# Splitting one weight unit in four with ScalarE and an adding DMA in a two-layer hybrid trunk

## The chip, the cores and the metric

The kernel runs on one core of one Trainium2 chip. A time is device microseconds of one execution. The profile is of one further execution, taken by the hardware profiler; its times are microseconds from its start. PE is TensorE, DVE is VectorE, ACT is ScalarE, POOL is GpSimd and SP is SyncE. SP, ACT and POOL can issue DMA transfers, which all run on the core's 16 DMA engines.

## What is computed

The reference is a trunk of two layers over 256 tokens of width 2048, all in float32. Each layer has one projection of the normalised input (2048 to 8208 columns), two groups of mixing heads on its results, an output projection, and a gate on a second, small projection:

```python
for l in range(DEPTH):                       # DEPTH = 2, D_MODEL = 2048, SEQ = 256
    hn = rms_norm(h, norm_w[l])
    proj = hn @ w_in[l]                      # 2048 x 8208
    ...
    y = jnp.concatenate([y_a, y_b], axis=-1) # gated DeltaNet heads, HGRN2 heads
    h = h + y @ w_out[l]                     # 2048 x 2048
    gate = jax.nn.sigmoid(h @ w_ple_gate[l]) # 2048 x 2048
    h = h + (p[l] @ w_ple_up[l]) * gate      # 256 x 2048
return rms_norm(h, final_norm_w)
```

## The kernel before

**Products in three parts.** The matmuls use the type float32r, which keeps fewer bits than float32. So each operand x is split into a high part, x rounded to float32r, and a low part, x minus the high part. A product a times w is then the sum of three matmuls: a high by w high, a high by w low, a low by w high (`products`, L414 to L434). All accumulate in PSUM.

**Steps and units.** The weights are packed ahead in the order in which they are used. One step of the plan (`make_plan`, L87) uses one weight unit: mostly two row blocks of 128 rows with 512 columns, which in SBUF are 128 partitions with 1024 float32 each (512 KB). A step is 12 matmuls of 128x512: two row blocks, two halves of 128 tokens, three parts. There are 392 steps, 196 a layer. In layer 0, steps 0 to 127 are the input projection ("in"), 128 to 159 the output projection ("out"), 160 to 195 the gate projection ("gate") with one step of the small projection ("up") in each of its four chunks of 512 columns. Layer 1 is the same from step 196 on. The first two chunks of a stage take turns, four row blocks each; the third and fourth follow one after the other.

**How a unit is made.** `load` (L374) lets SP issue the transfer from HBM into a tile `raw` of the pool `wraw` (three buffers). `prep` (L387) lets ACT write the high part `whi` (L400) and DVE the low part `wlo` (L402), into pools of three buffers each. `ahead` (L405) runs in program order before each step n: it asks for loads up to four units ahead, limited to three more than have been prepared, and for parts up to two units ahead. So ACT can write unit n's high part when the step three units earlier has been done, and a `raw` buffer comes free when DVE has read it.

**What sets the order.** The matmuls and transposes on PE are kept in the program's order. On the other engines a scheduler orders the instructions when the program is built; each engine then works through its own queue in that order, waiting on semaphores. After each step the mixing heads' next pieces are run from a table of delays (`tick`, L358), and those of `after_out` (L1163) and `after_gate` (L1169) when a chunk of the out or gate stage is done. `after_gate` makes the sigmoid of a chunk's gate on ACT and DVE (L1172, L1174, L1176, L1177), adds to h on DVE (L1179, L1180) and takes sums of squares on ACT (L555). In the last layer POOL multiplies h by the final norm's weight (L1183).

**Buffers that the change borrows.** The pool `mix` has a tag "et" (two tiles of 1024 float32 on each partition), which holds the evicted results of the input projection until they are transposed (`evict`, L593), and at the start the transposed input. Its tag "Bt" (one tile of 2048) holds the matrices of the DeltaNet heads that are inverted (`Inverse`, L612). Neither is written between the end of one input projection's work and the next one.

Of the kernel before, what the change touches and what calls it, by code (L numbers as in the profile page):

```python
# [8 lines left out]
F32 = mybir.dt.float32  # L9
F32R = mybir.dt.float32r  # L10
I32 = mybir.dt.int32
AF = mybir.ActivationFunctionType
ALU = mybir.AluOpType
# [18 lines left out]
def chunk_cols(chunk):  # L32

    return [(START[k], 16) if k == "ba" else (START[k] + 256 * g, 256) for k, g in chunk]
# [52 lines left out]
def make_plan():  # L87

    steps, off = [], 0

    def add(what, l, c, cols, k, first, last):
        nonlocal off
        n = sum(w for _, w in cols)
        steps.append(dict(what=what, l=l, c=c, cols=cols, n=n, kts=k, off=off, first=first, last=last))
        off += 128 * n * len(k)

    for l in range(DEPTH):
        for what in ("in", "out", "gate"):
            chunks, order = stage_plan(what, l)
            for c, k4 in order:  # L100
                cols = chunk_cols(chunks[c]) if what == "in" else [(512 * c, 512)]
                w = 2 if sum(x for _, x in cols) > 272 else 4
                kts = OUT_KTS if what == "out" else tuple(range(KT))
                for q in range(0, 4, w):
                    last = k4[q + w - 1] == kts[-1]
                    end = l + 1 == DEPTH and c == 3
                    if what == "gate" and k4[q + w - 1] == KT - (9 if end else 1):
                        add("up", l, c, cols, (0, 1), True, True)
                    add(what, l, c, cols, k4[q:q + w], k4[q] == kts[0], last)
    return steps, off  # L110
# [56 lines left out]
def trunk(ctx: ExitStack, tc: tile.TileContext, head, xT, x, pT, W, par, fw, cst, msk, eye, out):  # L167
    nc = tc.nc
# [7 lines left out]
    mp = pool("mix", 1)  # L176
# [4 lines left out]
    V, S, G = nc.vector, nc.scalar, nc.gpsimd  # L181
# [187 lines left out]
    steps, _ = make_plan()  # L369
    raws, ready = {}, {}  # L370
    LOOK, LOAD = 2, 4
    state = dict(next=0, loaded=0, prepped=0)

    def load(n, after=None):  # L374
        s = steps[n]
        f = s["n"] * len(s["kts"])
        raw = raws[n] = wr.tile([128, 1088], F32, tag="raw", name=f"raw{n}")
        i = nc.sync.dma_start(out=raw[:, :f], in_=W[s["off"]:s["off"] + 128 * f].rearrange("(p f) -> p f", p=128))
        if n <= 17:
            tc.keep_in_program_order(i)  # L380
        if after is not None:
            tc.add_manual_dep(i.ins, after.ins.name, mybir.DependencyInfo(
                mybir.DependencyClass.Sync, mybir.DependencyReason.DATA), reason="later")
        if n in follow:
            follow[n]()

    def prep(n):  # L387
        s = steps[n]
        f = s["n"] * len(s["kts"])
        raw = raws.pop(n)  # L390
        if n >= len(steps) - 2:

            ready[n] = [split(raw[:, 512 * j:512 * j + 512], j, None, f"w{n}") for j in range(2)]
            return
        hi = ws.tile([128, 1088], F32R, tag="whi", name=f"whi{n}")
        lo = ws.tile([128, 1088], F32R, tag="wlo", name=f"wlo{n}")
        w = f // 4 if n < 2 else f
        parts = [slice(j, j + w) for j in range(0, f, w)]
        for sl in parts:
            S.activation(hi[:, sl], raw[:, sl], AF.Copy)  # L400
        for sl in parts:
            V.tensor_tensor(lo[:, sl], raw[:, sl], hi[:, sl].bitcast(F32), ALU.subtract)  # L402
        ready[n] = [(hi[:, j * s["n"]:(j + 1) * s["n"]], lo[:, j * s["n"]:(j + 1) * s["n"]]) for j in range(len(s["kts"]))]

    def ahead(n):  # L405
        while state["loaded"] < min(len(steps), n + 1 + LOAD) or state["prepped"] < min(len(steps), n + 1 + LOOK):
            if state["loaded"] < min(len(steps), n + 1 + LOAD, state["prepped"] + WRAW):
                load(state["loaded"])
                state["loaded"] += 1
            else:  # L410
                prep(state["prepped"])
                state["prepped"] += 1

    def products(n, m, psums, act, js=range(4), run=None, parts=range(3)):  # L414

        s = steps[n]
        if isinstance(psums[m], list):
            if run is None:
                products(n, m, psums, act, run=0)
                run = 1  # L420
            ps, cols = psums[m][run], RUNS[run]
        else:
            ps, cols = psums[m], slice(0, s["n"])
        for j, (hi, lo) in enumerate(ready[n]):
            if j not in js:
                continue
            kp, kj = divmod(s["kts"][j], 2)
            ah, al = (a[:, T * kj + 128 * m:T * kj + 128 * m + 128] for a in act[kp])
            o = ps[:, cols]
            for i, (a, b) in enumerate(((ah, hi), (ah, lo), (al, hi))):  # L430
                if i not in parts:
                    continue
                PE.matmul(o, a, b[:, cols], start=(s["first"] and j == 0 and i == 0),
                          stop=(s["last"] and j == len(ready[n]) - 1 and i == 2))  # L434

    def run_step(psums, act):

        n = state["next"]
        s = steps[n]
        ahead(n)  # L440
        if not n:
            for j in range(4):
                for i in (0, 2, 1):
                    for m in range(2):
                        products(n, m, psums, act, js=(j,), parts=(i,))
                if j == 1:
                    warm(1)
        for m in range(2):
            if n:
                products(n, m, psums, act)  # L450
        del ready[n]
        state["next"] = n + 1
        if s["what"] != "up":
            tick()
        return s
# [25 lines left out]
    def split(src, kp, scales, name):  # L481

        hi = ap_.tile([128, 2 * T], F32R, tag="ahi", name=f"{name}hi{kp}")
        lo = ap_.tile([128, 2 * T], F32R, tag="alo", name=f"{name}lo{kp}")
        if scales is None:
            S.activation(hi, src, AF.Copy)
            V.tensor_tensor(lo, src, hi.bitcast(F32), ALU.subtract)
            return hi, lo
        w = 2 * T // len(scales)
        for j, sc in enumerate(scales):  # L490
            S.activation(hi[:, w * j:w * j + w], src[:, w * j:w * j + w], AF.Copy, scale=sc)
        for j, sc in enumerate(scales):
            sl = slice(w * j, w * j + w)
            V.scalar_tensor_tensor(lo[:, sl], src[:, sl], sc, hi[:, sl].bitcast(F32), ALU.mult, ALU.subtract)
        return hi, lo
# [762 lines left out]
    for l in range(DEPTH):  # L1258
# [25 lines left out]
        for c, k4 in order:  # L1284
# [5 lines left out]
            w = 2 if sum(n for _, n in chunk_cols(ch)) > 272 else 4  # L1290
            for q in range(0, 4, w):
# [19 lines left out]
                s = run_step(ps[c], act)  # L1311
# [28 lines left out]
        for c, k4 in order:  # L1340
            if c not in ps:
                ps[c] = banks(f"gate{l}{c}", c)
                if l + 1 == DEPTH and c == 3:

                    ps[c][1] = [ps[c][1], pm.tile([128, 512], F32, tag="m", name="gaterun")]
            for q in (0, 2):
                end = l + 1 == DEPTH and c == 3
                if k4[q + 1] == KT - (9 if end else 1):
                    up = [pm.tile([128, 512], F32, tag="m", name=f"up{l}{c}{m}") for m in range(2)]
                    run_step(up, pact)  # L1350
                if end and k4[q + 1] == KT - 9:
                    break
                while not pairs_ready(hact, k4[q:q + 2]):
                    tick()
                run_step(ps[c], hact)
            if end and k4[3] == KT - 9:

                n = state["next"]
                for i in range(5):
                    ahead(n + i)  # L1360
                    products(n + i, 0, ps[c], hact)
                half0 = Finish(0, ps[c], up, st)
                for r in range(2):
                    for i in range(5):
                        products(n + i, 1, ps[c], hact, run=r)
                last_norm(half0, Finish(1, ps[c], up, st))
                break
            if k4[3] == KT - 1:
                spawn(after_gate(c, ps[c], up, act, st, l))
# [35 lines left out]
```

## Time and profile before

| what | value |
|---|---|
| three runs | 1246.13 us median, 1245.79 to 1248.45 |
| the profiled execution, first to last instruction | 1246.4 us; no other time of its own is given |
| mean granted TensorE clock | 0.996 |
| busy: PE, DVE, ACT, POOL | 1229.5, 880.0, 778.1, 69.5 us |
| out and gate stages of layer 0, in the trace | about 428 to 623 us |
| out and gate stages of layer 1, in the trace | about 1044 to 1237 us |
| bytes moved by DMA | 218.71 MB, 175 GB/s in the mean |

A group of instructions in the profile is a line with its engine, its operation and the tiles out<-in, the count after an x, then the busy time in us and the mean of one in ns, then the idle time of that engine just before them with what ended it. A row of the timeline has the start, the duration, the engine, the line and the operation. A row of the chain of waits has the start, the duration, and the engine and tile that the end of the program depended on in that time. Rows of a table by stretches have the busy time of PE, weight loads, DVE, ACT and POOL, the granted clock, the busy share of the DMA engines and GB/s.

### The profile page before, as it was taken

The page shows a single profiled execution, that of the slowest core. Times are in us where ns is not written, and L with a number is a line of the kernel's source. Part 1 is how long each engine was busy: PE and PEld are TensorE (multiplying, and loading weights), DVE is VectorE, ACT ScalarE, POOL GpSimd, SP SyncE. Part 2 cuts the span into 40 slices and gives each one's busy share as a digit, 9 for nine tenths or more (in the row PEclk, how much of TensorE's full clock was granted, in tenths as well). Part 3 has the DMA queues.
Part 4 walks back from the last instruction along what each step waited for, and adds up shares of the span by engine and source line. Part 5 has one row for each costly group of instructions (what it writes and reads, how often), then busy time and mean ns, then how long its engine had stood idle before and what let it go on. Part 6 is the DMA issues. An engine that isn't in the chain of part 4 may idle for free.

```text
span 1246.4 us, 21626 instructions
## 1 busy us (share of the span) xinstructions
PE 1229.5 (99%) x8385; PEld 1033.1 (83%) x8385; DVE 880.0 (71%) x1520; ACT 778.1 (62%) x1397; POOL 69.5 (6%) x64
## 2 busy tenths in 40 slices
PE   9999999999999999999999999999999999999996
PEld 7888887798888888888888888887888888888886
DVE  7777796878568656547567778977876695565566
ACT  7676776586757744437556768674766576444464
POOL 0310000000000000000003100000000000000010
PEclk9999999999999999999999999999999999999998
DMA  8555555435464445555555555555445555656563
GB/s 288 174 178 175 174 174 160 170 122 187 152 219 153 170 177 184 187 186 186 187 184 170 174 178 165 177 175 154 134 140 165 172 156 185 207 179 181 183 203 135
DMA packets 73719, 218.71 MB, mean 175 GB/s; under 512 B 15504, under 2 KB 20752, under 8 KB 73616
## 3 DMA queue, kind: packets, MB, share of 16 engines
q1 hardware_dynamic: 63392, 211.78, 52.0%
q10 hardware_dynamic: 10224, 5.54, 1.5%
q8 instruction: 66, 1.08, 0.3%
q14 instruction: 37, 0.30, 0.1%
HBM read 212.84 MB, written 4.46 MB: 174 GB/s over the span
## 4 chain that ended last, share of the span: by engine, by line
PE 89%; DVE 6%; ACT 2%; DMA 1%; issue 1%; SPq 0%; DVEq 0%; ACTq 0%
PE out L336 14%; PE gate L336 14%; PE in1hf L336 7%; PE in0dk L336 7%; PE in0dv L336 6%; PE in1dv L336 6%; PE in1dk L336 6%; PE in1hi L336 6%; PE in0hf L336 5%; PE in0hi L336 4%; DVE wlo L402 2%; PE up L336 2%; PE in1dz L336 1%; PE in0dz L336 1%; ACT whi L400 1%
## 5 line engine op out<-in xcount | busy, mean ns | idle before, releaser
L402 DVE TENSOR_TENSOR wlo<-raw,whi 128x1024 fp32r<-128x1024 f32 (+1 forms) x392 | 483.0, 1234 | 273.9 <-ACT whi L400 272.7
L400 ACT ACTIVATE whi<-raw 128x1024 fp32r<-128x1024 f32 (+1 forms) x392 | 411.6, 1051 | 328.2 <-PE out L336 90.8
L336 PE MATMUL in1hf<-whi,n1hi 128*128 128x512 f32 x128 | 51.0, 398 | 0.9 <-issue 0.9
L336 PE MATMUL in1hi<-whi,n1hi 128*128 128x512 f32 x128 | 51.6, 403 | 0.0
L336 PE MATMUL in1dk<-whi,n1hi 128*128 128x512 f32 x128 | 51.3, 401 | 0.0
L336 PE MATMUL in1hi<-wlo,n1hi 128*128 128x512 f32 x128 | 50.0, 391 | 0.7 <-DVE wlo L402 0.7
L336 PE MATMUL gate<-whi,g0hi 128*128 128x512 f32 x128 | 50.1, 392 | 0.0
L336 PE MATMUL in1dk<-wlo,n1hi 128*128 128x512 f32 x128 | 50.0, 391 | 0.1
L336 PE MATMUL in1hi<-whi,n1lo 128*128 128x512 f32 x128 | 50.0, 391 | 0.0
L336 PE MATMUL in1dk<-whi,n1lo 128*128 128x512 f32 x128 | 50.0, 390 | 0.0
L336 PE MATMUL in1hf<-whi,n1lo 128*128 128x512 f32 x128 | 49.9, 390 | 0.0
L336 PE MATMUL in1hf<-wlo,n1hi 128*128 128x512 f32 x128 | 49.9, 390 | 0.0
L336 PE MATMUL gate<-whi,g0lo 128*128 128x512 f32 x128 | 49.8, 389 | 0.0
L336 PE MATMUL gate<-wlo,g0hi 128*128 128x512 f32 x128 | 49.8, 389 | 0.0
L336 PE MATMUL in1dv<-whi,n1hi 128*128 128x512 f32 (+1 forms) x128 | 48.1, 376 | 0.0
L336 PE MATMUL in1dv<-whi,n1lo 128*128 128x512 f32 (+1 forms) x128 | 46.5, 364 | 0.0
L336 PE MATMUL in1dv<-wlo,n1hi 128*128 128x512 f32 (+1 forms) x128 | 46.5, 363 | 0.0
L336 PE MATMUL gate<-whi,g1hi 128*128 128x512 f32 (+1 forms) x120 | 45.5, 379 | 0.0
L336 PE MATMUL gate<-wlo,g1hi 128*128 128x512 f32 (+1 forms) x120 | 45.4, 379 | 0.0
L336 PE MATMUL gate<-whi,g1lo 128*128 128x512 f32 (+1 forms) x120 | 45.4, 378 | 0.0
L336 PE MATMUL in0hi<-wlo,n0hi 128*128 128x512 f32 x96 | 38.3, 399 | 2.0 <-DVE wlo L402 2.0
L336 PE MATMUL in0hi<-whi,n0hi 128*128 128x512 f32 x96 | 39.3, 410 | 0.0
(1495 smaller groups left out, 3172.8 us busy)
## 6 DMA issues: line engine op xcount, KB each, us to landing
raw<-W SPq DMA_DIRECT2D x384, 512.0 KB, 3.5
raw<-W SPq DMA_DIRECT2D x7, 544.0 KB, 3.7
h<-x SPq DMA_DIRECT2D x4, 512.0 KB, 4.7
xt<-xT SPq DMA_DIRECT2D x3, 512.0 KB, 5.9
out_dram<-h SPq DMA_DIRECT2D x6, 256.0 KB, 2.2
di0d<-di0Bt ACTq DMA_DIRECT2D x4, 256.0 KB, 2.7
di1d<-di1Bt ACTq DMA_DIRECT2D x4, 256.0 KB, 2.3
fw<-fw ACTq DMA_DIRECT2D x2, 512.0 KB, 5.5
```

The lines of the kernel that those rows point to most:

```text
L336: return tc.keep_in_program_order(nc.tensor.matmul(*a, **k))
L400: S.activation(hi[:, sl], raw[:, sl], AF.Copy)
L402: V.tensor_tensor(lo[:, sl], raw[:, sl], hi[:, sl].bitcast(F32), ALU.subtract)
```

## The change

Every unit n of the out and gate products with n % 4 == 2 is made another way, except in the last eight steps: units 130, 134, up to 190 (16 of them) and 326, 330, up to 382 (15 of them). Its raw weights are loaded into a tile of the tag "et", and both parts go into one tile of the tag "Bt". ACT writes the negative of the high part into the place of the low part, then POOL issues a transfer from the raw tile to that place which adds (`accum_op=ALU.add`), so that raw minus high part remains there. ACT then writes the high part as well. DVE has no part in such a unit. `far_prep(n)` is called right after the preparation of unit n-1, so before the matmuls of step n-3.

```diff
+    def by_dma(n):
+
+        s = steps[n]
+        return s["what"] in ("out", "gate") and n % 4 == 2 and n < len(steps) - 8
+
+    def far_load(n):
+
+        raw = raws[n] = mp.tile([128, 1024], F32, tag="et", name=f"raw{n}", bufs=2)
+        s = steps[n]
+        nc.sync.dma_start(out=raw, in_=W[s["off"]:s["off"] + 128 * 1024].rearrange("(p f) -> p f", p=128))
+
+    def far_prep(n):
+
+        raw = raws.pop(n)
+        w = mp.tile([128, 2048], F32R, tag="Bt", name=f"w{n}", bufs=1)
+        hi, lo = w[:, 0:1024], w[:, 1024:2048]
+        S.activation(lo, raw, AF.Copy, scale=-1.0)
+        G.dma_start(out=lo.bitcast(F32), in_=raw, accum_op=ALU.add)
+        S.activation(hi, raw, AF.Copy)
+        ready[n] = [(hi[:, 512 * j:512 * j + 512], lo[:, 512 * j:512 * j + 512]) for j in range(2)]
+
     def load(n, after=None):
         s = steps[n]
+        if by_dma(n):
+            return far_load(n)
...
             else:
-                prep(state["prepped"])
+                if not by_dma(state["prepped"]):
+                    prep(state["prepped"])
                 state["prepped"] += 1
+                if state["prepped"] < len(steps) and by_dma(state["prepped"]):
+                    far_prep(state["prepped"])
```

In the changed kernel the lines behind L411 stand 23 to 26 lines lower: `whi` is written at L423, `wlo` at L425, the negative high part at L390, the adding transfer is L391 and the high part of such a unit L392.

How this moves instructions, first on ACT in the out stage of layer 0, where nothing else stands between the units. The number behind a tile's name tells tiles apart; before, these rows are units 140 to 144:

```order
L400 ACTIVATE whi_5123<-raw_5085 128x1024
L400 ACTIVATE whi_5141<-raw_5103 128x1024
L400 ACTIVATE whi_5159<-raw_5121 128x1024
L400 ACTIVATE whi_5177<-raw_5139 128x1024
L400 ACTIVATE whi_5197<-raw_5157 128x1024
```

and after the change, with unit 142 in the tile w_5145:

```order
L423 ACTIVATE whi_5123<-raw_5089 128x1024
L423 ACTIVATE whi_5141<-raw_5103 128x1024
L390 ACTIVATE w_5145<-raw_5121 128x1024
L392 ACTIVATE w_5145<-raw_5121 128x1024
L423 ACTIVATE whi_5177<-raw_5139 128x1024
L423 ACTIVATE whi_5197<-raw_5161 128x1024
```

Unit 142 keeps its place on ACT and has two rows instead of one; its row on DVE is gone.

On ACT at the end of the gate stage's first chunk in layer 0, `pg` is the sigmoid of `after_gate` for the two halves of the tokens, and the units are 177 and 178. Before:

```order
L1172 ACTIVATE pg_5884<-gate_0_5590 128x512
L1176 ACTIVATE pg_5884<-pg_5884 128x512
L1172 ACTIVATE pg_5885<-gate_1_5591 128x512
L1177 ACTIVATE pg_5884<-pg_5884 128x512
L400 ACTIVATE whi_5904<-raw_5848 128x1024
L1176 ACTIVATE pg_5885<-pg_5885 128x512
L400 ACTIVATE whi_5924<-raw_5866 128x1024
L1177 ACTIVATE pg_5885<-pg_5885 128x512
```

After:

```order
L423 ACTIVATE whi_5904<-raw_5848 128x1024
L1198 ACTIVATE pg_5884<-gate_0_5594 128x512
L1202 ACTIVATE pg_5884<-pg_5884 128x512
L1198 ACTIVATE pg_5885<-gate_1_5595 128x512
L1203 ACTIVATE pg_5884<-pg_5884 128x512
L390 ACTIVATE w_5908<-raw_5866 128x1024
L1202 ACTIVATE pg_5885<-pg_5885 128x512
L392 ACTIVATE w_5908<-raw_5866 128x1024
L1203 ACTIVATE pg_5885<-pg_5885 128x512
```

Unit 177 has moved ahead of the sigmoid; unit 178's negative copy stands behind four of its rows, and its high part one row further on. Units 190 and 374 stand in the same way behind the end of a chunk.

On POOL's queue in the last layer, h_85, h_86 and h_87 are three of the four chunks of h and fw is the final norm's weight. Before:

```order
L590 TENSOR_TENSOR dn13sz<-dn13zs,dn13sz 128x512
L590 TENSOR_TENSOR hg13sz<-hg13zs,hg13sz 128x512
L1183 TENSOR_TENSOR h_85<-h_85,fw_11761 128x512 x2
L1183 TENSOR_TENSOR h_86<-h_86,fw_11761 128x512 x2
L1183 TENSOR_TENSOR h_87<-h_87,fw_11761 128x512 x2
```

After, where w_12085, w_12181 and w_12253 are units 374, 378 and 382:

```order
L391 DMA w_11991<-raw_11967 128x1024
L391 DMA w_12085<-raw_12041 128x1024
L1209 TENSOR_TENSOR h_85<-h_85,fw_11765 128x512 x2
L391 DMA w_12181<-raw_12157 128x1024
L1209 TENSOR_TENSOR h_86<-h_86,fw_11765 128x512 x2
L391 DMA w_12253<-raw_12229 128x1024
L1209 TENSOR_TENSOR h_87<-h_87,fw_11765 128x512 x2
```

The last two transfers are queued behind products with fw that wait for ACT's sums of squares.

## The prediction

> **What bounds the kernel now.** I read the page's busy times first, then the chain of waits in the stretches that the change touches, then a stretch of one step, then the transfers.
>
> ```profile
> span 1246.4 us, 21626 instructions
> PE 1229.5 (99%) x8385; PEld 1033.1 (83%) x8385; DVE 880.0 (71%) x1520; ACT 778.1 (62%) x1397; POOL 69.5 (6%) x64
> ```
>
> TensorE (PE) is idle for 16.9 us in all. The chain of waits says whether its busy time is a bound or only covers waits. First the out stage, then the gate stage of layer 0, then rows of layer 1's gate stage and of the end.
>
> ```profile
> by line: PE out L336 91.3%; PE g0t L339 2.4%; PE hg03po L336 1.9%; PE dn03pw L336 1.2%; PE dn03po L336 1.2%; PE dn03pS L336 0.6%; PE dn03pz L336 0.6%; PE hg03yp L339 0.6%; PE dn03yp L339 0.6%
> ...
> by line: PE gate L336 82.2%; PE up L336 12.8%; PE n1t L339 3.1%; PE in1dz L336 2.2%
> ...
> 560.65 5.44 PE gate L336 x24
> 566.09 2.72 PE up L336 x12
> 568.81 8.16 PE gate L336 x36
> ...
> 595.08 13.60 PE gate L336 x60
> ...
> 1184.29 21.76 PE gate L336 x96
> ...
> 1233.07 3.61 PE gaterun L336 x30
> 1236.70 0.39 ACT pg L1203
> ```
>
> Every name there is PE: a step of 12 matmuls takes 2.72 us and the next follows at once. VectorE (DVE) and ScalarE (ACT) end no wait of PE in these stages. So DVE's busy share of 71% is no measure of what relief there is worth.
>
> ```profile
> 485.26 0.39 PE L336 MATMUL out<-whi,dn01hi 128*128 128x512 f32 x1
> 485.46 1.06 ACT L400 ACTIVATE whi<-raw 128x1024 fp32r<-128x1024 f32 x1 [1.66 <-PE out L336]
> 485.49 0.39 PE L336 MATMUL out<-wlo,dn01hi 128*128 128x512 f32 x1
> ...
> 486.56 1.23 DVE L402 TENSOR_TENSOR wlo<-raw,whi 128x1024 fp32r<-128x1024 f32 x1 [1.49 <-ACT whi L400]
> ...
> 487.98 0.39 PE L336 MATMUL out<-whi,hg02hi 128*128 128x512 f32 x1
> 488.18 1.06 ACT L400 ACTIVATE whi<-raw 128x1024 fp32r<-128x1024 f32 x1 [1.66 <-PE out L336]
> ```
>
> A step starts at 485.26, the next at 487.98. ACT starts a high part 0.20 us after a step begins, because the step before has given a buffer back; DVE ends the low part at 487.79, and it is for the step after the next. Both engines then wait for PE.
>
> **What is removed: no time.** DVE loses 31 low parts (16 in layer 0, 15 in layer 1).
>
> ```profile
> L402 DVE TENSOR_TENSOR wlo<-raw,whi 128x1024 fp32r<-128x1024 f32 (+1 forms) x89 | 109.6, 1234 | 79.6 <-ACT whi L400 79.6
> L400 ACT ACTIVATE whi<-raw 128x1024 fp32r<-128x1024 f32 (+1 forms) x88 | 93.3, 1060 | 96.7 <-PE out L336 46.4 <-PE gate L336 35.1 <-PE up L336 5.2
> ```
>
> 31 x 1.234 = 38 us, all out of time in which DVE already ends early. PE's own instructions and their order stay, but for one transpose that comes one place away. Gain on the path: 0.
>
> **What is added on ScalarE: no time in a steady stretch.** 31 more activations of 1.06 us are 33 us. Per four units ACT then has 5 x 1.06 = 5.3 of 10.88 us.
>
> ```profile
> 500.00:520.00 20.00, 20.00 (x94) 16.66 (x93) 9.88 (x9) 8.46 (x10) 0.00 (x0) 1.00 0.52 187
> ```
>
> ACT is busy 8.46 of 20 us there, DVE 9.88. What hides it is the wait of 1.66 us before each high part, and the other units now share three buffers among three units in four, so each of them may start a step earlier than before. Without that cover each would cost PE up to 1.06 us.
>
> **What is added on the transfers: this decides.** The negative high part of a unit n can start when unit n-4 has been used, that is 0.20 us after step n-3 starts. It ends at 0.20 + 1.06 = 1.26. The low part is read by the second matmul of step n, at 3 x 2.72 + 0.23 = 8.39. So the transfer, from GpSimd's issue to landing, has 8.39 - 1.26 = **7.13 us**. In three units it has less: 178, 190 and 374. There the negative copy stands behind the gate's activations of the chunk that ended one step before (L1172, L1176, L1172, L1177).
>
> ```profile
> 562.05 0.60 ACT L1172 ACTIVATE pg<-gate 128x512 f32<-128x512 f32 x1 [0.30 <-PE gate L336]
> ...
> 564.39 0.62 ACT L1177 ACTIVATE pg<-pg 128x512 f32<-128x512 f32 x1
> 564.91 1.05 ACT L400 ACTIVATE whi<-raw 128x1024 fp32r<-128x1024 f32 x1
> ```
>
> It takes the place of the activation at 564.91 and ends at 565.97. Step 178 starts at 568.81 + 2.72 = 571.53, its second matmul 0.23 later: 571.76 - 565.97 = **5.79 us**.
>
> How long the transfer takes, L, no row shows: nothing here adds in a transfer, and nothing is issued from GpSimd (POOL). The nearest rows:
>
> ```profile
> L378 SPq DMA_DIRECT2D raw<-W x391: 327/328/1078, 3.6 to 1222.3; - x196
> ...
> DMA to landing us min/median/max: 2.9/3.5/6.0
> ...
> q1 hardware_dynamic: 63392, 211.78, 52.0%
> ...
> fw<-fw ACTq DMA_DIRECT2D x2, 512.0 KB, 5.5
> ...
> 50.59 2.27 POOL L590 TENSOR_TENSOR dn00sz<-dn00zs,dn00sz 128x512 f32<-128x512 f32 x1
> ...
> 328.44 1.27 POOL L590 TENSOR_TENSOR hg02sz<-hg02zs,hg02sz 128x512 f32<-128x512 f32 x1 [26.35 <-DVE wlo L402]
> ```
>
> - A load of the same 512 KB lands in 3.5 us (2.9 to 6.0) beside the same stream of loads.
> - The add reads what lies at its target as well, so I count the engines' time once more. The loads' queue took 0.520 x 1246.4 = 648 us of all 16 engines for 211.78 MB, so 1.60 us for 0.524 MB.
> - GpSimd's preparation: between the 0.33 us that SP takes to issue, and the 1.27 to 2.27 us of a GpSimd pass over 128 rows. I take 1.0, in the middle.
>
> L = 3.5 + 1.6 + 1.0 = **6.1 us**. Lower end: 2.9, if the second read and GpSimd cost nothing. Upper end: 6.0 + 1.6 + 2.27 = 9.9. The two loads of fw that went out together (5.5) lie near the middle.
>
> [...]
>
> With L = 6.1 a steady unit lands 1.0 us before it is needed. Units 178, 190 and 374 are late by 0.31 each: 3 x 0.31 = **0.9 us**.
>
> **Room on the 16 engines.** Per four units: 4 x 1.60 for the loads and 3.2 for the add, 9.6 of 10.88 us. PE itself isn't slowed by busy transfers:
>
> ```profile
> 18.64 5.45 PE in0dk L336 x24
> 27.11 5.45 PE in0dk L336 x24
> ...
> 626.20 5.45 PE in1dk L336 x24
> ...
> 20.00:40.00 20.00, 20.00 (x116) 17.70 (x115) 15.14 (x31) 11.14 (x17) 1.94 (x4) 1.00 0.71 248
> ```
>
> Two steps took 5.45 us with the engines 71% busy as they did later at about 55%.
>
> **Queues.** On SP's queue each load into the borrowed tag "et" waits for the transfer of two such units earlier. Behind it stand ordinary loads (unit 143's behind unit 146's). Unit 138's transfer must have landed by step 138 anyway, and a load takes 3.5 us while unit 143 is five steps (13.6 us) away: nothing. On GpSimd's queue, unit 378's transfer stands behind two products with the final weight.
>
> ```profile
> 1186.80 1.46 POOL L1183 TENSOR_TENSOR h<-h,fw 128x512 f32<-128x512 f32 x1 [1.38 <-PE gate L336]
> ```
>
> They end at 1188.26; unit 378's negative copy can't start before step 375, at 1184.29 + 2 x 2.72 = 1189.73: nothing.
>
> **Sum.** 0 + 0 + 0.9. The profiled execution spans 1246.4 us, the median of the three runs is 1246.13, so the span stands for the time: 1246.13 + 0.9 = 1247.0. A measurement of this kernel can tell 0.2%, 2.5 us, from no change.
>
> **The rivals.**
>
> - *Forecast: the low parts land in time* (L below 6.6). PE stays the only name on the chain. 2.5 us are reached at 3 x (L - 5.79) = 2.5, L = 6.6. Range 1245.5 to 1248.6. For it: the load's 3.5 us leave 3.6 us for all that is unknown. Chance 0.55.
> - *Slower: every unit lands late.* PE waits in each fourth step for the transfer. From L = 7.13 on, 28 x (L - 7.13) + 3 x (L - 5.79); between 6.6 and 7.13 only the three units, 2.5 to 4 us. At L = 8: 24.4 + 6.6 = 31, so 1277. At 9.9: 78 + 12 = 90, so 1336. For it: some loads took 6.0 us with no second read. Against: those are the longest of 391. Chance 0.30, of which 0.11 beyond L = 8.
> - *Slower: GpSimd is held up by VectorE.* The same product on GpSimd took 1.27 and 2.27 us. If preparing a transfer waits out a low part on DVE (1.23), L is 7.33: 28 x 0.20 + 3 x 1.54 = 10.2, so 1256. Chance 0.06. [...]
> - *Slower: the transfer engines are full.* If adding runs at a quarter of the load's rate, it takes 6.4 us, and four units 12.8 instead of 10.88: 31 x 1.92 = 60, so 1306. It decides from 10.88 - 6.4 = 4.5 us of engine time. Chance 0.05.
> - *Faster.* VectorE's 38 us would have to shorten a wait of PE, and the chain has none in these stages. What is left is the tail from 1236.7 to the end, 9.7 us, whose work is the same; a gain of a third of it would give 1243. Chance 0.04.
>
> **The numbers.** Forecast 1247.0. Slower: 0.30 + 0.06 + 0.05 = 0.41; same 0.55; faster 0.04. For the range I leave out L beyond 8 (0.11), full engines (0.05) and most of the gain (0.03), 0.19 in all: 1245.5 to 1277.
>
> **What would show it.** Right: in the profile after, the out and gate stages' chain names only PE; steps still take 2.72 us; from GpSimd's issue to landing about 6 us; no idle time of PE behind a DMA but at three units; DVE's busy time down by 38 us and ACT's up by 33. Wrong: PE idle before the second matmul of a unit n with n % 4 == 2, with the transfer as releaser, 28 times or more; a landing above 7.13 us; loads that land later than 6 us; or DVE among the names on the chain.

## The result, and the profile after

The changed kernel takes 1249.74 us (median of 9 runs, 1247.52 to 1252.37), the kernel before 1245.74 us beside it (median of 9, 1243.40 to 1248.45). The ratio is 1.0029, with a 95% interval of 1.0018 to 1.0040: slower by 3.6 us, 2.2 to 5.0. The interval excludes a change of zero; its lower end lies just under the 2.5 us that the prediction takes as the least that can be told. The profiled execution of the kernel after spans 1249.8 us.

The page of the kernel after, first the span and the engines' busy times, then the queues of the loads and of the adding transfers (packets, MB, share of the 16 engines' span):

```profile
span 1249.8 us, 21690 instructions
...
PE 1233.3 (99%) x8385; PEld 1034.4 (83%) x8385; DVE 846.5 (68%) x1489; ACT 806.4 (65%) x1428; POOL 97.2 (8%) x95
...
q1 hardware_dynamic: 63392, 211.78, 50.7%
q0 software_dynamic: 4464, 16.25, 6.7%
```

VectorE has lost 33.5 us and ScalarE gained 28.3, as intended (38 and 33 were forecast by adding durations up; where two instructions overlap, the busy time counts once). But PE is busy for 3.8 us longer with the same 8385 matmuls, and it is idle for 16.5 us, where it was 16.9. The mean granted clock is 0.995, where it was 0.996. So what was lost isn't a wait: the matmuls themselves have become slower.

The adding transfers, asked for by their line: the time of GpSimd's instruction (min/median/max in ns), who waited for it, and the time from issue to landing.

```profile
L391 POOL DMA_DIRECT2D w<-raw x31: 850/869/1013, 412.5 to 1205.1; - x31
...
who waited for it (us, times):
  PEld gate L336: 0.5, 2
...
DMA to landing us min/median/max: 4.5/5.1/7.1
```

All but two land in time. PE's loads of 128x128 blocks (PEld) waited for two of 31, 0.5 us in all, both in layer 1's gate stage (units 374 and 378). Most of that wait was hidden behind matmuls already under way: the steps of these two units are 0.11 and 0.07 us longer than those of other borrowed units, 0.17 together.

The chain of waits in the same stretches as before, layer 0's gate stage and then layer 1's (start, us, what, matmuls):

```profile
563.13 5.53 PE gate L336 x24
568.66 2.72 PE up L336 x12
571.38 8.26 PE gate L336 x36
...
597.82 13.74 PE gate L336 x60
...
1186.95 22.12 PE gate L336 x96
```

The chain names PE alone, as before. But 24 matmuls take 5.53 us instead of 5.44, 60 take 13.74 instead of 13.60, and 96 in layer 1, which hold the two late units, take 22.12 instead of 21.76. The x12 of the step between stays at 2.72.

Which steps are longer is seen in PE's rows. In these matmuls (`products`) the weight unit is the wide operand, 128x512 in a row; the 128x128 that PEld loads are activations. Here are the first matmuls of three steps in a row, in the kernel after: the step that reads the borrowed tile w, and the two behind it.

```profile
495.34 0.64 PE L336 MATMUL out<-w,dn03hi 128*128 128x512 f32 x2
...
498.10 0.40 PE L336 MATMUL out<-whi,hg03hi 128*128 128x512 f32 x1
...
500.87 0.39 PE L336 MATMUL out<-whi,hg00hi 128*128 128x512 f32 x1
```

The step on w takes 2.76 us and the next, an ordinary one, 2.77. From then on it is 2.72 again (from the trace's starts in ns, the median of each place in the period of four: 2.763, 2.770, 2.720, 2.720). The excess begins and ends with a step. It is 0.093 us for each of 31 units, 2.9 us at most (the expectations below count 0.095). The out and gate stages together, measured below, are 2.9 us longer, the late landings included. The rest of the 3.4 us between the two spans lies outside these stages and is not placed. The question for the experiments was why two steps of four are slow.

### The profile page after: what moved, and what is told of

Its sections match the earlier page's. It is cut to its first block, busy times and chain, and to the rows that moved or that the text cites. A ratio compares the mean times of both kernels' runs of the same rounds, so it can differ in the third digit from the quotient of the medians.

```text
span 1249.8 us, 21690 instructions
## 1 busy us (share of the span) xinstructions
PE 1233.3 (99%) x8385; PEld 1034.4 (83%) x8385; DVE 846.5 (68%) x1489; ACT 806.4 (65%) x1428; POOL 97.2 (8%) x95
## 3 DMA queue, kind: packets, MB, share of 16 engines
q1 hardware_dynamic: 63392, 211.78, 50.7%
## 4 chain that ended last, share of the span: by engine, by line
PE 90%; DVE 6%; ACT 2%; DMA 1%; issue 1%; SPq 0%; DVEq 0%; ACTq 0%
PE out L336 14%; PE gate L336 14%; PE in1hf L336 7%; PE in0dk L336 7%; PE in1dk L336 6%; PE in0dv L336 6%; PE in1dv L336 6%; PE in1hi L336 6%; PE in0hf L336 5%; PE in0hi L336 4%; DVE wlo L425 2%; PE up L336 2%; DMA raw<-W 1%; PE in1dz L336 1%; PE in0dz L336 1%
## 5 line engine op out<-in xcount | busy, mean ns | idle before, releaser
L425 DVE TENSOR_TENSOR wlo<-raw,whi 128x1024 fp32r<-128x1024 f32 (+1 forms) x361 | 446.7, 1239 | 284.7 <-ACT whi L423 283.2
L423 ACT ACTIVATE whi<-raw 128x1024 fp32r<-128x1024 f32 (+1 forms) x361 | 378.7, 1051 | 262.3 <-PE out L336 51.4
L390 ACT ACTIVATE w<-raw 128x1024 fp32r<-128x1024 f32 x31 | 32.8, 1058 | 42.5 <-PE out L336 25.4
L391 POOL DMA_DIRECT2D w<-raw x31 | 27.0, 872 | 286.7 <-ACT w L390 248.9
L336 PE MATMUL in0hf<-whi,n0hi 128*128 128x512 f32 x96 | 38.4, 400 | 0.0
L336 PE MATMUL in0dk<-whi,n0hi 128*128 128x512 f32 x96 | 38.3, 399 | 0.0
L336 PE MATMUL in0hi<-whi,n0lo 128*128 128x512 f32 x96 | 38.0, 396 | 0.0
L336 PE MATMUL gate<-whi,g0hi 128*128 128x512 f32 x96 | 37.9, 395 | 0.0
```

What stands on the lines that cost most here:

```text
L336: return tc.keep_in_program_order(nc.tensor.matmul(*a, **k))
L390: S.activation(lo, raw, AF.Copy, scale=-1.0)
L391: G.dma_start(out=lo.bitcast(F32), in_=raw, accum_op=ALU.add)
```

## The experiments

One stretch serves for all: 96 matmuls of the out stage of layer 0, eight steps, which hold two of the changed units. It is one piece of the chain, in the kernel before and in the kernel after:

```profile
479.97 21.78 PE out L336 x96
```

```profile
481.78 21.98 PE out L336 x96
```

Two units cost 0.20 us there, 0.10 each. The whole of out and gate is told by the timeline: from the first out matmul to the first of layer 1's in stage, and in layer 1 to PE's last. These are 196.36 and 194.55 us before, 390.9 together; 197.75 and 196.02 after, 393.8.

**dve_low: the borrowed tiles without the transfer.**

```
-        S.activation(lo, raw, AF.Copy, scale=-1.0)
-        G.dma_start(out=lo.bitcast(F32), in_=raw, accum_op=ALU.add)
         S.activation(hi, raw, AF.Copy)
+        V.tensor_tensor(lo, raw, hi.bitcast(F32), ALU.subtract)
```

> The low part of every fourth out and gate unit is made by VectorE (1.23 us each) again, but raw, high and low part stay in the borrowed tiles (tags et and Bt). No negative copy, no adding transfer. What is to be explained: in the kernel after, the step that reads the borrowed tile takes 2.764 us and the step behind it 2.771, against 2.720 of the others, 0.095 us per unit, 31 units, 2.9 us. Theory 'transfer' (the adding transfer and the loads that bunch behind it slow TensorE): both steps back to 2.720, time 1245.7 to 1246.5. Theory 'place' (TensorE reads the borrowed tile more slowly, wherever its data come from): the reading step stays near 2.76 and the next near 2.77, time 1248.5 to 1249.5. Theory 'ScalarE' (two activations one behind the other in the step behind the reading one): the reading step and the next lose most of their excess, time 1246 to 1247.

1248.0 us against 1245.36, ratio 1.0018 (1.0007 to 1.0029). Out and gate took 393.6 us. The chain's piece:

```profile
480.83 21.98 PE out L336 x96
```

Without any adding transfer and with no added work on ScalarE the stretch takes the 21.98 us of the kernel after, and the two steps 2.763 and 2.770 us. 'Transfer' and 'ScalarE' are out: the price belongs to the borrowed tile. The whole time, 1248.0, lies between the ranges of the theories, half a microsecond under that of 'place'; the steps decide. Out and gate are 0.2 us shorter than in the kernel after, as much as the two late landings cost there.

**add_unread: the transfer without the borrowed tile.**

```
         S.activation(hi, raw, AF.Copy)
-        ready[n] = [(hi[:, 512 * j:512 * j + 512], lo[:, 512 * j:512 * j + 512]) for j in range(2)]
+        raws[n] = raw
...
-                if not by_dma(state["prepped"]):
-                    prep(state["prepped"])
+                prep(state["prepped"])
```

> Negative copy, adding transfer and high part are made in the borrowed tile as in the kernel after, but nobody reads them: the unit's high and low part are also made in ordinary buffers by ScalarE and VectorE, and TensorE reads those. Theory 'transfer': TensorE is slowed as in the kernel after, about 0.09 us per unit, 1248.5 to 1250. Theory 'place': all steps 2.720 us, time 1245.7 to 1247 (ScalarE then has 4 x 1.06 + 2 x 1.06 = 6.4 of 10.88 us, which stays covered). Theory 'ScalarE': the step with the two extra activations stays slow, about 0.05 us per unit, 1247 to 1248.

1252.68 us, ratio 1.0053 (1.0041 to 1.0065): slower than any theory had it. The chain's piece, one row in it, and then PE's wait and a window behind it in layer 1's gate stage (PE busy, PEld, DVE, ACT, POOL, then the granted clock and the DMA share):

```profile
480.63 21.84 PE out L336 x96
```

```profile
500.88 0.45 PE L336 MATMUL out<-whi,hg00hi 128*128 128x512 f32 x1
```

```profile
PE gate L336 <- DVE wlo L425: 1.7, 1, 1.7
```

```profile
1200.00:1206.00 6.00, 6.00 (x23) 4.85 (x22) 3.78 (x3) 1.75 (x2) 1.47 (x1) 0.82 0.46 160
```

The steps are back at 2.720 us; the 0.06 that is left of 21.84 stands at the one matmul shown, 0.45 us long where its neighbours take 0.39. The time went mostly to one place that this experiment made itself: with two extra activations per unit, a high part and then its low part came late behind a chunk's end in layer 1, PE waited once, and behind the wait the granted clock was 0.82. That one step took 6.41 us, 3.7 more. Layer 1's out and gate took 198.95 us, 4.4 more than before; layer 0's only 0.5 more. For the whole time the run shows nothing about the borrowed tile. For the steps it agrees with dve_low.

**shift64 and shift192: the borrowed tile further on.** As built, Bt's tile starts at byte 176960 of each partition, 64 beside a multiple of 128, and in both experiments too. The six ordinary buffers all start at multiples of 256, and so do, in every kernel here, the activations that these matmuls read.

```
-        w = mp.tile([128, 2048], F32R, tag="Bt", name=f"w{n}", bufs=1)
-        hi, lo = w[:, 0:1024], w[:, 1024:2048]
+        w = mp.tile([128, 2064], F32R, tag="Bt", name=f"w{n}", bufs=1)
+        hi, lo = w[:, 16:1040], w[:, 1040:2064]
```

In shift192 the tile has 2096 elements, and the parts are w[:, 48:1072] and w[:, 1072:2096].

> As the kernel after, but the borrowed tile is 16 elements wider and high and low part start 64 bytes further on in each partition, so that they start at a multiple of 128 bytes, as the six ordinary buffers do; in the kernel after they start 64 bytes beside one. Theory 'place' in the form that this offset matters: steps back to 2.720 us, time 1245.7 to 1246.8. Theory 'place' by the tile itself, theory 'transfer' and theory 'ScalarE': no change, 1249 to 1250.

> As the kernel after, but the borrowed tile is 48 elements wider and high and low part start 192 bytes further on: at multiples of 256 bytes, as all six ordinary buffers do (shift64 reached multiples of 128 only, and its reading step took 2.789 us). High and low part stay 4096 bytes apart, where those of an ordinary unit are 13056 apart. Theory 'offset' (TensorE reads a tile more slowly that doesn't start at a multiple of 256 bytes): reading step and the next back to 2.720 us, time 1245.5 to 1246.5. Theory 'distance' (what matters is how far apart the two parts lie that TensorE reads in turn): reading step stays above 2.75 us, time 1248.5 to 1250.

shift64: 1249.65 us, ratio 1.0032 (1.0021 to 1.0042), nothing won; its reading steps took 2.792 us and the steps behind them 2.735. So a multiple of 128 bytes, on which this expectation rested, is not enough. shift192: 1246.19 us, ratio 1.0001 (0.9992 to 1.0010), the loss is gone within that interval. The chain's piece of shift64, then of shift192:

```profile
481.95 21.95 PE out L336 x96
```

```profile
478.27 21.78 PE out L336 x96
```

And shift192's first matmuls of the same three steps:

```profile
491.72 0.61 PE L336 MATMUL out<-w,dn03hi 128*128 128x512 f32 x2
...
494.44 0.39 PE L336 MATMUL out<-whi,hg03hi 128*128 128x512 f32 x1
...
497.16 0.39 PE L336 MATMUL out<-whi,hg00hi 128*128 128x512 f32 x1
```

2.72 and 2.72. All 31 transfers, the negative copies and the bunched loads are still there. 192 bytes in the place of a tile were the price of the change in its steps. What is left is one late landing: for unit 378 PEld waited 0.8 us and the step took 3.40 us, 0.68 more; layer 1's out and gate took 195.39 us, 0.8 more than before.

**ordinary_64 and ordinary_4096: the kernel before, its own buffers laid out otherwise.** Nothing is borrowed or added here. In the first all out and gate units start 64 bytes into their buffers:

```
         lo = ws.tile([128, 1088], F32R, tag="wlo", name=f"wlo{n}")
+        if s["what"] in ("out", "gate"):
+            hi, lo = hi[:, 16:], lo[:, 16:]
```

In the second both parts of a unit lie in one buffer, as they do in Bt (unit 0's are made in the same way):

```
-        hi = ws.tile([128, 1088], F32R, tag="whi", name=f"whi{n}")
-        lo = ws.tile([128, 1088], F32R, tag="wlo", name=f"wlo{n}")
+        both = ws.tile([128, 2176], F32R, tag="whi", name=f"whi{n}")
+        hi, lo = both[:, 0:f], both[:, f:2 * f]
```

> The kernel before with nothing borrowed, but in every out and gate unit (some 64 in a layer) high and low part start 64 bytes into their ordinary buffers, 13056 bytes apart as before. Theory 'offset': each of these steps takes about 2.764 us instead of 2.720: 128 x 0.044 = 5.6 us, with transitions up to 7, time 1250.5 to 1252.5. Theory 'distance': 2.720 us a step, time 1245 to 1246.

> The kernel before with nothing borrowed, but high and low part of a unit are two parts of one buffer, 4096 bytes apart (4352 in the units of 1088 elements), each start at a multiple of 256 bytes. Theory 'distance': steps of out and gate take 2.75 to 2.79 us instead of 2.720, 128 x 0.03 to 0.07 = 4 to 9 us there alone, time over 1249. Theory 'offset': no change, 1245 to 1246.

ordinary_64: 1248.91 us, ratio 1.0024 (1.0012 to 1.0037). ordinary_4096: 1244.88 us, ratio 0.9995 (0.9985 to 1.0005). The pieces, in that order:

```profile
478.72 21.99 PE out L336 x96
```

```profile
477.65 21.78 PE out L337 x96
```

'Distance' is out, 'offset' holds, in buffers that were never borrowed. But its size was wrong: eight moved steps cost 0.21 us, 0.026 each (2.747 us from start to start, 0.027 more) and not 0.044. Two moved steps among ordinary ones had cost as much.

**quarter_64, half_64 and ordinary_128: how many units are moved, and how far.** The same edit with n % 4 == 2 or n % 2 == 0 as a further condition, and for all units with 32 elements in place of 16:

```
+        if n % 4 == 2 and s["what"] in ("out", "gate"):
+            hi, lo = hi[:, 16:], lo[:, 16:]
```

> The kernel before with nothing borrowed, but in every fourth out and gate unit alone (32 to 33 units) high and low part start 64 bytes into their ordinary buffers. In ordinary_64, where all 128 such units were moved, a step settled at 2.744 us instead of 2.720, 0.024 each, and the time rose by 3.5 us. Theory 'change of offset' (a step that is read at another offset than the step ahead of it runs slower, and so does the next, 0.095 us for the pair as in the kernel after): 32 x 0.095 = 3.0 us, 1248 to 1249, as much as all 128 together, and the patterns of the kernel after (2.764 and 2.771 us). Theory 'each moved step costs the same': 32 x 0.024 = 0.8 us, 1245.5 to 1246.5. Theory 'borrowed tile' (the pair's price belongs to the tile Bt): steps of 2.744 and 2.720 us.

> As quarter_64, but every second out and gate unit starts 64 bytes into its buffers. Theory 'change of offset': 64 x 0.095 = 6.1 us, 1250.5 to 1252.5, more than when all units are moved. Theory 'each moved step costs the same': 64 x 0.024 = 1.5 us, 1246 to 1247.5.

> As ordinary_64, but all out and gate units start 128 bytes into their ordinary buffers. In shift64 the step that read the borrowed tile 128 bytes beside a multiple of 256 took 2.789 us, 0.069 more. If a step that is at the same offset as its neighbours settles as with 64 bytes, 128 x 0.02 to 0.03 = 3 to 4 us, 1248 to 1249.5; if 128 bytes cost by themselves what the single step showed, 128 x 0.069 = 8.8 us, 1253 to 1255; if only an offset of 64 within 128 bytes costs once the neighbours agree, 1245 to 1246.

quarter_64: 1249.3 us against 1245.94, ratio 1.0027 (1.0015 to 1.0039). half_64: 1250.21 us, 1.0039 (1.0024 to 1.0054). ordinary_128: 1254.14 us, 1.0068 (1.0051 to 1.0085). The first two lie 0.3 us beside the ranges of 'change of offset', above and below, and far from those of the other theory; the third lies in that of 128 bytes that cost by themselves. The three pieces:

```profile
481.27 21.98 PE out L336 x96
```

```profile
478.01 22.14 PE out L336 x96
```

```profile
481.16 22.31 PE out L336 x96
```

| kernel | units off a multiple of 256 in the stretch | the stretch, us | out and gate, us over before's 390.9 |
|---|---|---|---|
| before | 0 of 8 | 21.78 | 0 |
| after | 2, by 64 bytes | 21.98 | 2.9 |
| shift192 | 0 (2 in the borrowed tile) | 21.78 | 0.8 |
| dve_low | 2, by 64 | 21.98 | 2.7 |
| shift64 | 2, by 128 bytes | 21.95 | 3.0 |
| quarter_64 | 2, by 64 | 21.98 | 2.7 |
| half_64 | 4, by 64 | 22.14 | 5.1 |
| ordinary_64 | 8, by 64 | 21.99 | 3.5 |
| ordinary_128 | 8, by 128 | 22.31 | 8.2 |

'Change of offset' holds. A quarter of the units at 64 bytes costs as much as all of them, half of them costs more than all (the ratios' intervals of half_64 and ordinary_64 overlap, but the stretches, 22.14 and 21.99, are plain). quarter_64 is the kernel before with the same 31 units moved by 64 bytes, and it repeats the stretch of the kernel after to 0.01 us and its two steps to 0.001. At 128 bytes it is otherwise: every step costs (22.31 - 21.78) / 8 = 0.066 us, even where all neighbours agree, and a lone one (shift64) costs 0.072 itself and only 0.015 in the step behind it.

**late_neg: what a late transfer costs.** The negative copy is held back behind the high part of unit n+1:

```
-            S.activation(hi[:, sl], raw[:, sl], AF.Copy)
+            state["hi"] = S.activation(hi[:, sl], raw[:, sl], AF.Copy)
...
-        S.activation(lo, raw, AF.Copy, scale=-1.0)
+        i = S.activation(lo, raw, AF.Copy, scale=-1.0)
+        tc.add_manual_dep(i.ins, state["hi"].ins.name, mybir.DependencyInfo(
+            mybir.DependencyClass.Sync, mybir.DependencyReason.DATA), reason="later")
...
                     prep(state["prepped"])
                 state["prepped"] += 1
-                if state["prepped"] < len(steps) and by_dma(state["prepped"]):
-                    far_prep(state["prepped"])
+                if by_dma(state["prepped"] - 2):
+                    far_prep(state["prepped"] - 2)
```

> As the kernel after, but ScalarE makes the negative copy only behind the high part of the unit after the next (unit n+1), which waits for the buffer of unit n-3: it starts one step later, at 0.20 + 1.06 us into step n-2 instead of 0.20 into step n-3, and the transfer's budget falls from 7.13 to 5.44 + 0.23 - 2.32 = 3.35 us. The prediction's rival 'every unit lands late', with the landing of 5.1 us that the kernel after shows: TensorE waits 5.1 - 3.35 = 1.75 us in front of the second matmul of each such unit, 31 x 1.75 = 54 us, 1298 to 1308. If a late transfer costs less than what it is late by (another unit's work could fill in, or it lands sooner), under 1280.

1386.25 us, ratio 1.1117 (1.1089 to 1.1144): 141 us, not 54. Its busy line; PE's waits for the transfers; two rows of one unit's step; a window behind that wait; and the transfers' landing times:

```profile
PE 1278.7 (92%) x8385; PEld 1059.5 (76%) x8385; DVE 844.9 (61%) x1489; ACT 809.8 (58%) x1428; POOL 96.3 (7%) x95
```

```profile
PE gate L336 <- DMA w<-raw: 47.8, 15, 4.1
PE out L336 <- DMA w<-raw: 45.1, 16, 3.4
```

```profile
526.36 0.40 PE L336 MATMUL out<-w,dn00hi 128*128 128x512 f32 x1
529.22 0.51 PE L336 MATMUL out<-w,dn00hi 128*128 128x512 f32 x1 [2.46 <-DMA w<-raw]
```

```profile
529.20:532.00 2.80, 2.78 (x8) 2.19 (x9) 0.00 (x0) 0.00 (x0) 0.00 (x0) 0.67 0.61 222
```

```profile
DMA to landing us min/median/max: 4.7/6.4/8.0
```

PE waits in front of the second matmul of all 31 units, 92.9 us together, 3.0 each. The place and the cause are those of the rival; the price had two terms missing. The transfers land after 6.4 us instead of 5.1. Around the one shown SP issued two loads (from late_neg's timeline), while in the kernel after SP mostly stands and waits for the transfer (from SP's waits there):

```profile
522.58 3.05 SPq L403 DMA_DIRECT2D raw<-W  x2
522.74 0.86 POOL L393 DMA_DIRECT2D w<-raw  x1 [13.66 <-ACT w L390]
```

```profile
SPq L383 <- DMA w<-raw: 173.5, 27, 8.3
```

That the loads beside it make the landing longer fits these rows, but was not tried by itself. And behind such a wait the granted clock was 0.67 in the window shown. Apart from the end of the program, the trace's record of the clock has it at one half in 22 stretches, 95.6 us in all, where the kernel after has one stretch of 3.4. The mean granted clock is 0.963 here and 0.995 there. Half of 95.6 is 47.8, and PE is busy for 45.4 us more than in the kernel after. 92.9 + 45.4 = 138.3, and the spans differ by 1387.5 - 1249.8 = 137.7.

## Why the prediction was right and wrong

The range of 1245.5 to 1277 held the time of 1249.74, but by luck. The case that the prediction held likeliest, "the low parts land in time", ends at 1248.6; the range went on from there for transfers that land late, and late landings cost 0.17 us. Of the mechanism, what it says of waits is what runs: PE alone is on the chain in these stages and nearly every low part is in time. What it says of PE's steps is not. Its time of 1247.0 was 2.7 us too low.

- **What bounds the kernel** was read rightly: PE, step behind step. VectorE's 33.5 us bought nothing; shift192, which has the change without its side effect, measures 1.0001.
- **ScalarE's copies** cost nothing in the steady stretches, as said: 28.3 us more, hidden in its waits (shift192's stretch takes 21.78 us with all of them).
- **The landing.** 6.1 us was estimated, 5.1 (4.5 to 7.1) was measured. GpSimd's part was estimated at 1.0 and is 0.87. The engines' time was estimated at 3.2 and is 0.067 x 1249.8 / 31 = 2.7, where the loads' queue, at 0.507 of the same span for 211.78 MB, takes 1.6 for as many bytes. The second read was the prediction's estimate; no run shows it by itself. The sum leaves out 0.4 us from the end of the negative copy to the start of GpSimd's instruction; with it, 5.5 of the 7.13 us are used. The steady units are in time, as forecast.
- **The short units** were sized at 0.9 us. Measured: 0.17 us of longer steps in the kernel after, for units 374 and 378, and 0.68 in shift192, for 378 alone. 178 and 190 landed 0.8 and 0.9 us before their use, and of 378 the prediction had said "nothing". GpSimd's queue indeed didn't hold 378 up, but ScalarE's did: its negative copy stands behind activations of the sigmoid and started at 1194.39, 2.0 us after step 375 and not 0.20.

```profile
1193.35 1.13 ACT L1203 ACTIVATE pg<-pg 128x512 f32<-128x512 f32 x2
1194.39 1.04 ACT L390 ACTIVATE w<-raw 128x1024 fp32r<-128x1024 f32 x1
...
1195.84 0.87 POOL L391 DMA_DIRECT2D w<-raw  x1 [5.00 <-ACT w L390]
...
1200.80 0.19 PEld L336 LDWEIGHTS gate<-w,g1hi 128*128 128x128 f32 x1 [0.24 <-DMA w<-raw]
```

- **SP's queue** was called free. SP waits 173.5 us for the transfers, far from free for SP, but shift192, with the same queue, has its steps at 2.72 us.
- **"PE itself isn't slowed by busy transfers"** holds: shift192 has all of them at 2.72 us a step. Its DMA engines are busy for 0.80 of the stretch where those of the kernel before are for 0.55, and both take 21.78 us.
- **The step that failed** stands under "What is removed": "PE's own instructions and their order stay, ... Gain on the path: 0". The instructions stay, but 31 of the steps read their weights from another place, 64 bytes beside a multiple of 128, and here a matmul's time was not independent of that. The term that is missing from the sum is 0.09 us for each of 31 units, 2.7 us in the stages of dve_low and quarter_64, which have no adding transfer. The sign "steps still take 2.72 us" is where the profile after shows it wrong, on the 31 steps that read the tile and on the steps behind them. None of the rivals was this one: all slower ones were waits, and here PE waits no longer than before.
- **The rivals.** Late units: two in the kernel after, at 0.17 us; late_neg shows that the mechanism is real and costs more than lateness alone: 92.9 us of waits and 45.4 us more of PE's busy time, with the granted clock at one half in 22 stretches. GpSimd held up by VectorE: in the kernel after no low part runs beside its instruction, but in add_unread eight do, and there it took 852 to 903 ns, as it does alone (850 to 1013 in the kernel after); so no. Full engines: no, at 2.7 us a transfer.

Why the start of the weights in a partition matters to a matmul, and why the step behind one that starts elsewhere is slow too, no run here shows. Nor is it separated whether the high or the low part's place counts, and no other offsets than 64 and 128 bytes were tried. What is shown is that place alone does it (the stretch takes 21.98 us in dve_low and in quarter_64, 21.78 before), and that moving the tile to a multiple of 256 bytes takes it away with the transfers and copies unchanged (21.78 us in shift192). No version was faster than the kernel before by more than its interval.

## What to carry to other kernels

When a change puts a matmul's wide operand in another tile, compare the start of that tile within the partition with those of the tiles that it stands beside in the stream; a borrowed tile has whatever start the pool gave it. Here a start 64 bytes beside a multiple of 256 cost 0.093 us a unit, and one at such a multiple left the steps at 2.72 us (shift192). In a kernel that is bound by PE, count PE's busy time for the same number of matmuls before and after: if it grew and nobody waits, look at the start-to-start times of steps, not at waits. And the 33.5 us that were taken off VectorE, which ended no wait of PE in the out and gate stages, bought nothing, even in shift192, where the steps cost nothing more (ratio 1.0001).

## What the runs showed of the hardware that was not expected

- Matmuls in float32r whose 128x512 operand started at a multiple of 256 bytes followed each other every 226.7 ns (2.720 us for twelve, in the kernel before and in shift192). With all units 64 bytes into their buffers it was 0.026 us more per step of twelve (ordinary_64), with 128 bytes 0.066 us (ordinary_128).
- Where a step at 64 bytes stood among steps at 0, it took 0.043 us more and the next 0.050 (quarter_64); at 128 bytes 0.072 and 0.015 (shift64).
- An adding transfer of 512 KB inside SBUF, issued by GpSimd, took 0.87 us of GpSimd, 2.7 us of the 16 engines, and 5.1 us to landing in the kernel after; 6.4 us to landing in late_neg.
- Behind a wait of PE of 2.5 us the granted clock over the next 2.8 us was 0.67 (late_neg); behind a wait of 1.7 us that ended at 1198.15 it was 0.82 from 1200 to 1206 (add_unread).
